# RWKV-7 recurrence in a hybrid block: v centred by the product that turns it, the two heads' u in two PSUM banks

## The chip, the cores and the metric

The kernel runs on one core of a Trainium2 chip. The metric is the device time of one execution in microseconds (us). A core has five engines that work side by side, each through its own instructions in order: PE (TensorE, matmuls; its weight loads are shown apart as PEld), DVE (VectorE), ACT (ScalarE), POOL (GpSimd) and SP (SyncE, which issues most loads). PE writes only to PSUM, which has eight banks; DVE and ACT read PSUM and copy results to SBUF.

## The reference, cut to what matters

The kernel computes a whole encoder block for 512 positions of 1024 channels: an input projection, an RWKV-7 branch and a gated linear recurrence side by side, their merge, attention over a fixed memory and a gated convolutional feed-forward network. The change lies in the RWKV-7 branch. It has 8 heads of 64 channels, and per head a state S of 64x64 that is carried from position to position:

```
state = state * w_t + sa b_t^T + v_t k_t^T        with sa = state a_t
y_t   = state r_t
mean  = mean(y); var = mean((y - mean)^2)
y     = (y - mean) * rsqrt(var + eps) * lnx_g + lnx_b
```

Since y loses its mean over the 64 value channels directly afterwards, the kernel takes the mean out of v before the recurrence, and no mean of y is computed.

## The kernel before

The 512 positions are worked in 8 chunks of 64. The 8 heads stand as 4 pairs (`NPAIR`, index j); of a pair, head e = 0 lies in partitions 0 to 63 and head e = 1 in 64 to 127 (`half[e]`). For a chunk c, all within-chunk products of keys, queries and the inverse of the chunk's triangular system have been prepared in `AK` and `BZ`. What is left is a chain from chunk to chunk (`chunk`):

- `UV` holds for each head, stacked over the partitions, the state in one half and the centred v in the other. `x` = `UV` times `AK` (L756), copied by DVE to `Xs` (L759).
- `u` = `BZ` times `Xs` (L769). It replaces the state in `UV`: for head 0 by an ACT copy (L771), for head 1 by a DVE copy (L772).
- `s` = `KBr` times `UV` (L778) and a second part of `y` (L783; the first, L763, needs `x`'s operands only).
- `Sn` is `s` with its decay (L788); `Sn` plus the decayed old state goes into the next chunk's `UV` (L792), and the next `x` may start. `SP` prepares the decay one chunk ahead (L799).

Beside the chain, `rows_v` turns the next chunk's v from channels to rows, so that it can stand in `UV`: for head 0 by four products with the identity (L729), for head 1 by four transposes (L727), into one PSUM tile in bank "kv". DVE sums each row (`vm`, L731) and subtracts the mean while it copies into `UV` (two instructions, L734). `rows_kb` turns the keys (`kbr`, L743), in bank "kv" for head 0 and bank "s" for head 1, and ACT copies them (L744). The recurrence has four PSUM banks of its own: "kv", "xu" (x, then u), "y" and "s".

The order of the instructions of each engine is worked out when the program is built, by a planner with expected durations. The recurrence has the highest priority there, and where it is expected to wait, PE is given products of the input projection (`in_ps`, L160 to L162, each 512 columns wide) that are left. `pin` (`keep_in_program_order`) keeps the DVE instructions of the chain in the order of the code. In the finished program each engine takes its instructions in that order, and an instruction waits for its operands. Between the recurrence's products stand also the gates of the linear recurrence (`ga` and `gx`, L850, L852) and products of the group norm (`gv`, `gg`). When projection and recurrence are done, `yb_ps` follows.

An f32 product that isn't a transpose appears in the trace as two records on PE, a transpose as one. So the 8 products of `u` are "x16", and four products of v "x8".

Of the kernel before, what the change touches and what calls it, by code (L numbers as in the profile page):

```python
# [9 lines left out]
F32 = mybir.dt.float32  # L10
F32R = mybir.dt.float32r
AF = mybir.ActivationFunctionType
ALU = mybir.AluOpType
AX = mybir.AxisListType
# [3 lines left out]
P = 128  # L18
# [5 lines left out]
HD = 64  # L24
NC = T // HD
NPAIR = NH // 2
# [27 lines left out]
def hybrid_block_kernel(ctx: ExitStack, tc: tile.TileContext, xT_d, mT_d, pv_d, cst_d, win_d, wk_d, wv_d,  # L54
                        lup_d, gup_d, rga_d, rgx_d, wba_d, wbb_d, wmix_d, wq_d, wo_d, wfi_d, wfo_d, out_d):
    nc = tc.nc
    V, S, PE = nc.vector, nc.scalar, nc.tensor
# [12 lines left out]
    def mm_ps(name):  # L70
        return pmm.tile([P, T], F32, tag="mm", name=name)

    def rw_ps(name, pool=None, tag="rw", **kw):
        return (pool or prw).tile([P, T], F32, tag=tag, name=name, **kw)
# [4 lines left out]
    ident = cst[:, 0:P]  # L79
    bones = cst[:, P:2 * P]  # L80
    smask = cst[:, 2 * P:2 * P + T]
    scmask = cst[:, 2 * P + T:]
# [184 lines left out]
    with tc.tile_pool(name="p0", bufs=1, reuse_waits="tile") as p0:  # L267
# [36 lines left out]
        for m in range(KB):  # L304
            ps = rw_ps(f"k_ps{m}") if 3 <= m < 6 else mm_ps(f"k_ps{m}")
# [174 lines left out]
    BZ = pa.tile([P, NPAIR * NC, P], F32, tag="AR", name="BZ")  # L480
    KBt = big.tile([P, NPAIR, 2 * NC + 1, HD], F32, tag="x16", name="KBt")
    vT = pa.tile([P, NPAIR, T], F32, name="vT")
# [23 lines left out]
    half = (slice(0, HD), slice(HD, P))  # L506
# [25 lines left out]
    for i in range(2):  # L532
        hs, oh = half[i], half[1 - i]
# [137 lines left out]
    for e in range(2):  # L671
        o = HD * e
# [5 lines left out]
    for g in range(4):  # L678
        e, i0 = divmod(16 * g, 32)
        o = HD * e  # L680
# [8 lines left out]
        for i in range(16):  # L689
            PE.matmul(pso[o:o + 32, i * 32:(i + 1) * 32], Hs[k:k + 32, i, :], ZA[k:k + 32, 1 - e, i0 + i, :],  # L690
                      start=True, stop=True)
        V.tensor_copy(BZ[o:o + 32, i0:i0 + 16, 32:64], pso[o:o + 32].rearrange("p (i t) -> p i t", t=32))
    for e in range(2):
        o = HD * e
# [9 lines left out]
    ch = ch_ctx.enter_context(tc.tile_pool(name="ch", bufs=1, reuse_waits="tile"))  # L704

    gup = ch.tile([P, T], F32, name="gup")
    nc.scalar.dma_start(gup, gup_d)


    yT = vT  # L710
    j3 = lambda a: a.rearrange("p (j i) -> p j i", i=HD)
    pin = tc.keep_in_program_order

    def ch_ps(name, tag):
        return pch.tile([P, T], F32, tag=tag, name=name)

    def rows_v(c):

        UV = ch.tile([P, 2, NPAIR, HD], F32, tag="UV", name=f"UV{c}", bufs=2)
        ps = ch_ps(f"vr{c}", "kv")  # L720
        for e in range(2):
            hs, oh = half[e], half[1 - e]
            for j in range(NPAIR):
                o = ps[oh, j * HD:(j + 1) * HD]
                src = vT[hs, j, c * HD:(c + 1) * HD]
                if e:
                    PE.transpose(o, src, ident[hs, hs])  # L727
                else:
                    PE.matmul(o, src, ident[hs, hs], start=True, stop=True)  # L729
        vm = ch.tile([P, NPAIR], F32, tag="vm", name=f"vm{c}", bufs=2)  # L730
        pin(V.tensor_reduce(vm, j3(ps[:, 0:256]), AX.X, ALU.add))  # L731
        for e in range(2):
            oh = half[1 - e]
            pin(V.scalar_tensor_tensor(UV[oh, e], vm[oh].unsqueeze(2).to_broadcast([HD, NPAIR, HD]), -1.0 / HD,  # L734
                                       j3(ps[oh, 0:256]), ALU.mult, ALU.add))
        return UV

    def rows_kb(c):
        KBr = ch.tile([P, 2, NPAIR, HD], F32, tag="KBr", name=f"KBr{c}", bufs=2)
        for e in range(2):  # L740
            ps = ch_ps(f"kbr{c}_{e}", ("kv", "s")[e])
            for j in range(NPAIR):
                PE.transpose(ps[:, j * HD:(j + 1) * HD], kb_cols(j, e, c), ident[half[e], half[e]])  # L743
            S.copy(KBr[:, e], j3(ps[:, 0:256]))  # L744
        return KBr

    def pc_b(c):
        return PC[:, :, c].unsqueeze(2).to_broadcast([P, NPAIR, HD])

    def chunk(c, UV, KBr, SP):  # L750
        last = c == NC - 1
        nUV = nKB = None
        psx = ch_ps(f"x{c}", "xu")
        for j in range(NPAIR):
            for e in range(2):
                PE.matmul(psx[half[e], j * HD:(j + 1) * HD], AK[:, e, j * NC + c, 0:HD], UV[:, e, j, :],  # L756
                          start=True, stop=True)
        Xs = ch.tile([P, NPAIR, HD], F32, tag="Xs", name=f"Xs{c}", bufs=2)
        pin(V.tensor_copy(Xs, j3(psx[:, 0:256])))  # L759
        psy = ch_ps(f"y{c}", "y")  # L760
        for j in range(NPAIR):
            for e in range(2):
                PE.matmul(psy[half[e], j * HD:(j + 1) * HD], UV[:, e, j, :], AK[:, e, j * NC + c, HD:P],  # L763
                          start=(j == 0), stop=False)
        psu = ch_ps(f"u{c}", "xu")
        for j in range(NPAIR):
            for e in range(2):
                hs = half[e]
                PE.matmul(psu[hs, j * HD:(j + 1) * HD], BZ[hs, j * NC + c, 0:HD], Xs[hs, j, :],  # L769
                          start=True, stop=True)  # L770
        S.copy(UV[half[0], 0], j3(psu[half[0], 0:256]))  # L771
        pin(V.tensor_copy(UV[half[1], 1], j3(psu[half[1], 0:256])))  # L772
        if not last:
            nUV = rows_v(c + 1)
            pss = ch_ps(f"s{c}", "s")
            for j in range(NPAIR):
                for e in range(2):
                    PE.matmul(pss[half[e], j * HD:(j + 1) * HD], KBr[:, e, j, :], UV[:, e, j, :],  # L778
                              start=True, stop=True)
        for j in range(NPAIR):  # L780
            for e in range(2):
                hs = half[e]
                PE.matmul(psy[hs, j * HD:(j + 1) * HD], UV[hs, e, j, :], BZ[hs, j * NC + c, HD:P],  # L783
                          start=False, stop=(j == NPAIR - 1))
        if not last:
            nKB = rows_kb(c + 1)
            Sn = ch.tile([P, NPAIR, HD], F32, tag="Sn", name=f"Sn{c}", bufs=2)
            pin(V.tensor_tensor(Sn, j3(pss[:, 0:256]), pc_b(c), ALU.mult))  # L788
            for e in range(2):
                hs = half[e]  # L790
                if c:
                    pin(V.tensor_tensor(nUV[hs, e], Sn[hs], SP[hs], ALU.add))  # L792
                else:
                    pin(V.tensor_copy(nUV[hs, e], Sn[hs]))
        if c < NC - 2:
            SP = ch.tile([P, NPAIR, HD], F32, tag="SP", name=f"SP{c}", bufs=2)
            for e in range(2):
                hs = half[e]
                V.tensor_tensor(SP[hs], nUV[hs, e], pc_b(c + 1)[hs], ALU.mult)  # L799
        S.copy(yT[:, :, c * HD:(c + 1) * HD], j3(psy[:, 0:256]))  # L800
        return nUV, nKB, SP

    with tc.high_priority(offset=1000000):
        UV, KBr, SP = rows_v(0), rows_kb(0), None
        for e in range(2):
            V.memset(UV[half[e], e], 0.0)
        for c in range(NC):
            UV, KBr, SP = chunk(c, UV, KBr, SP)
# [142 lines left out]
    for m in range(KB):  # L951
        xin = pm.tile([P, T], F32, tag="xin", name=f"xin{m}")
        nc.scalar.dma_start(xin, xT_d[:, m, :])
        ps = mm_ps(f"mix_ps{m}")
# [115 lines left out]
    for m in order:  # L1070
        ps = mm_ps(f"co_ps{m}")
# [87 lines left out]
    for m0 in range(0, FB, NQ):  # L1159
# [25 lines left out]
        for m in ms:  # L1185
            s = pc.tile([P, T], F32, tag="s", name=f"fs{m}")
# [228 lines left out]
```

## Time and profile before

| | |
|---|---|
| median of three runs | 916.9 us (916.62 to 917.09) |
| the profiled execution | 917.18 us, of which the span of the program is 915.4 |
| granted TensorE clock, mean | 0.997 of full speed |
| busy share of the span | PE 98%, PEld 85%, DVE 76%, ACT 55%, POOL 14% |
| DMA | 200 MB, 219 GB/s on average |

A busy share is a mean over the whole span. PE's records overlap, so that PE counts as busy also where its products are spaced wider than they need to be; the start times and the chain show that, not the share.

### The profile page before, as it was taken

The page shows a single profiled execution, that of the slowest core. Times are in us where ns is not written, and L with a number is a line of the kernel's source. Part 1 is how long each engine was busy: PE and PEld are TensorE (multiplying, and loading weights), DVE is VectorE, ACT ScalarE, POOL GpSimd, SP SyncE. Part 2 cuts the span into 40 slices and gives each one's busy share as a digit, 9 for nine tenths or more (in the row PEclk, how much of TensorE's full clock was granted, in tenths as well). Part 3 has the DMA queues.
Part 4 walks back from the last instruction along what each step waited for, and adds up shares of the span by engine and source line. Part 5 has one row for each costly group of instructions (what it writes and reads, how often), then busy time and mean ns, then how long its engine had stood idle before and what let it go on. Part 6 is the DMA issues. An engine that isn't in the chain of part 4 may idle for free.

```text
span 915.4 us, 15846 instructions
## 1 busy us (share of the span) xinstructions
PE 896.7 (98%) x6186; PEld 777.7 (85%) x6186; DVE 695.9 (76%) x1119; ACT 505.2 (55%) x763; POOL 129.5 (14%) x159
## 2 busy tenths in 40 slices
PE   6999999999999999999999999999999999999996
PEld 6888877788867677787887778999999999999996
DVE  7884698767956687776566568789897889999674
ACT  7674666532335465333454456666565556767663
POOL 0102222010012211001111211111111111201100
PEclk9999999999999999999999999999999999999998
DMA  8778889576499975558878958899989998998962
GB/s 277 281 268 224 182 235 209 167 185 182 138 218 246 186 170 128 181 188 221 226 216 204 183 134 194 234 272 271 260 251 290 262 302 249 250 274 212 280 199 92
DMA packets 102410, 200.06 MB, mean 219 GB/s; under 512 B 25344, under 2 KB 36736, under 8 KB 102272
## 3 DMA queue, kind: packets, MB, share of 16 engines
q1 hardware_dynamic: 69504, 119.75, 40.1%
q0 software_dynamic: 25504, 67.38, 36.0%
q10 hardware_dynamic: 7328, 11.92, 3.8%
q8 instruction: 48, 0.79, 0.3%
q14 instruction: 26, 0.21, 0.1%
HBM read 187.75 MB, written 77.59 MB: 290 GB/s over the span
## 4 chain that ended last, share of the span: by engine, by line
PE 81%; DVE 9%; DMA 6%; ACT 2%; issue 1%; SPq 0%; DVEq 0%; ACTq 0%
PE in_ps L160 5%; PE in_ps L161 5%; PE in_ps L162 5%; PE fx_ps L160 5%; PE fx_ps L162 5%; PE fx_ps L161 5%; PE fyz_ps L160 3%; PE fyz_ps L162 3%; PE fyz_ps L161 3%; DMA wfo_r<-dOs 2%; PE mix_ps L160 2%; PE co_ps L160 2%; PE mix_ps L161 2%; PE mix_ps L162 2%; PE co_ps L162 2%; DMA Nm<-dM 2%
## 5 line engine op out<-in xcount | busy, mean ns | idle before, releaser
L126 ACT CAST wfi_h<-wfi_r 128x1024 fp32r<-128x1024 f32 x77 | 81.0, 1052 | 78.1 <-PE fx_ps L161 23.8
L160 PE MATMUL in_ps<-hT,win_h 128*128 128x512 f32 x304 | 122.6, 404 | 0.8 <-DVE pr L525 0.6
L161 PE MATMUL in_ps<-hT,win_h 128*128 128x512 f32 x304 | 122.0, 403 | 0.0
L162 PE MATMUL in_ps<-hT,win_l 128*128 128x512 f32 x304 | 121.1, 399 | 0.0
L127 DVE TENSOR_TENSOR wfi_l<-wfi_r,wfi_h 128x1024 fp32r<-128x1024 f32 x77 | 94.0, 1221 | 23.9 <-ACT wfi_h L126 23.8
L425 POOL DMA_DIRECT2D dS<-in_wfi x66 | 66.6, 1038 | 271.9 <-PE in_ps L160 125.4
L114 ACT CAST win_h<-win_r 128x1024 fp32r<-128x1024 f32 x38 | 39.8, 1048 | 72.8 <-PE in_ps L161 64.7
L115 DVE TENSOR_TENSOR win_l<-win_r,win_h 128x1024 fp32r<-128x1024 f32 x38 | 46.4, 1221 | 32.1 <-ACT win_h L114 32.1
L160 PEld LDWEIGHTS in_ps<-hT,win_h 128*128 128x128 f32 x304 | 57.0, 187 | 15.5 <-DVE pr L525 1.1
L161 PEld LDWEIGHTS in_ps<-hT,win_h 128*128 128x128 f32 x304 | 57.0, 188 | 14.5 <-issue 1.2
L162 PEld LDWEIGHTS in_ps<-hT,win_l 128*128 128x128 f32 x304 | 57.0, 187 | 14.1 <-issue 0.5
L461 POOL DMA_DIRECT2D dOs<-in_wfo x54 | 40.0, 800 | 185.9 <-PE fx_ps L160 51.4
L1242 DVE TENSOR_TENSOR wfo_l<-wfo_r,wfo_h 128x1024 fp32r<-128x1024 f32 (+1 forms) x39 | 47.1, 1208 | 14.1 <-ACT wfo_h L1241 13.9
L1241 ACT CAST wfo_h<-wfo_r 128x1024 fp32r<-128x1024 f32 (+1 forms) x39 | 40.4, 1038 | 28.3 <-PE oyz_ps L161 9.5
L160 PE MATMUL fx_ps<-hq,wfi_h 128*128 128x256 f32 x176 | 49.8, 283 | 0.0
L162 PE MATMUL fx_ps<-hr,wfi_l 128*128 128x256 f32 x176 | 49.7, 283 | 0.0
L160 PE MATMUL fx_ps<-hr,wfi_h 128*128 128x256 f32 x176 | 49.7, 282 | 0.0
L160 PE MATMUL ox_ps<-go,wfo_h 128*128 128x256 f32 x176 | 49.6, 282 | 0.0
L160 PE MATMUL fyz_ps<-hq,wfi_h 128*128 128x256 f32 x176 | 49.4, 281 | 0.0
L161 PE MATMUL fx_ps<-hr,wfi_h 128*128 128x256 f32 x176 | 49.4, 280 | 0.0
L162 PE MATMUL ox_ps<-go,wfo_l 128*128 128x256 f32 x176 | 49.3, 280 | 0.1
L161 PE MATMUL ox_ps<-go,wfo_h 128*128 128x256 f32 x176 | 49.3, 280 | 0.0
(418 smaller groups left out, 2728.8 us busy)
## 6 DMA issues: line engine op xcount, KB each, us to landing
dS<-in_wfi POOLq DMA_DIRECT2D x66, 512.0 KB, 8.3
wfi_r<-dS SPq DMA_DIRECT2D x44, 512.0 KB, 6.4
win_r<-in_win SPq DMA_DIRECT2D x38, 512.0 KB, 5.0
wfi_r<-in_wfi SPq DMA_DIRECT2D x33, 512.0 KB, 5.6
dS<-dS POOLq DMA_DIRECT2D x22, 512.0 KB, 6.0
dOs<-in_wfo POOLq DMA_DIRECT2D x12, 512.0 KB, 7.4
wv_r<-in_wv SPq DMA_DIRECT2D x8, 512.0 KB, 5.2
dG<-gs ACTq DMA_DIRECT2D x16, 256.0 KB, 3.0
```

What stands on the lines that cost most here:

```text
L114: S.copy(hi[:, o:o + n], raw[:, o:o + n])
L115: V.tensor_tensor(lo[:, o:o + n], raw[:, o:o + n], hi[:, o:o + n].bitcast(F32), ALU.subtract)
L126: S.copy(hi, raw)
L127: V.tensor_tensor(lo, raw, hi.bitcast(F32), ALU.subtract)
L160: first = PE.matmul(ps, lh, rh, start=start, stop=False, **kw)
L161: PE.matmul(ps, lh, rl, start=False, stop=False, **kw)
L162: PE.matmul(ps, ll, rh, start=False, stop=stop, **kw)
L425: return lambda: nc.gpsimd.dma_start(s(out), src, **kw)
L461: yield lambda k=k, w=w, src=src: nc.gpsimd.dma_start(dO[n, m][:, k * P:(k + w) * P], src, **kw)
L1241: S.copy(hi[:, :n], raw[:, :n])
L1242: V.tensor_tensor(lo[:, :n], raw[:, :n], hi[:, :n].bitcast(F32), ALU.subtract)
```

## The change

Three edits. A matrix `centre` = identity - (1/64) x block of ones is built once by DVE, in place of the mask `scmask`, which is no longer needed by then. In `rows_v` both heads' v is multiplied by `centre` instead of being turned by the identity or a transpose; the result is turned and centred at once, and two ACT copies bring it to `UV`; the reduction `vm` and the two DVE instructions go. In `chunk`, `u` gets two PSUM tiles, head 0 in bank "xu" and head 1 in bank "s".

```diff
+    centre = scmask
+    V.scalar_tensor_tensor(centre, bones, -1.0 / HD, ident, ALU.mult, ALU.add)
...
         for e in range(2):
             hs, oh = half[e], half[1 - e]
             for j in range(NPAIR):
-                o = ps[oh, j * HD:(j + 1) * HD]
-                src = vT[hs, j, c * HD:(c + 1) * HD]
-                if e:
-                    PE.transpose(o, src, ident[hs, hs])
-                else:
-                    PE.matmul(o, src, ident[hs, hs], start=True, stop=True)
-        vm = ch.tile([P, NPAIR], F32, tag="vm", name=f"vm{c}", bufs=2)
-        pin(V.tensor_reduce(vm, j3(ps[:, 0:256]), AX.X, ALU.add))
+                PE.matmul(ps[oh, j * HD:(j + 1) * HD], vT[hs, j, c * HD:(c + 1) * HD], centre[hs, hs],
+                          start=True, stop=True)
         for e in range(2):
             oh = half[1 - e]
-            pin(V.scalar_tensor_tensor(UV[oh, e], vm[oh].unsqueeze(2).to_broadcast([HD, NPAIR, HD]), -1.0 / HD,
-                                       j3(ps[oh, 0:256]), ALU.mult, ALU.add))
+            S.copy(UV[oh, e], j3(ps[oh, 0:256]))
...
-        psu = ch_ps(f"u{c}", "xu")
+        psu = [ch_ps(f"u{c}_{e}", ("xu", "s")[e]) for e in range(2)]
         for j in range(NPAIR):
             for e in range(2):
                 hs = half[e]
-                PE.matmul(psu[hs, j * HD:(j + 1) * HD], BZ[hs, j * NC + c, 0:HD], Xs[hs, j, :],
+                PE.matmul(psu[e][hs, j * HD:(j + 1) * HD], BZ[hs, j * NC + c, 0:HD], Xs[hs, j, :],
                           start=True, stop=True)
-        S.copy(UV[half[0], 0], j3(psu[half[0], 0:256]))
-        pin(V.tensor_copy(UV[half[1], 1], j3(psu[half[1], 0:256])))
+        S.copy(UV[half[0], 0], j3(psu[0][half[0], 0:256]))
+        pin(V.tensor_copy(UV[half[1], 1], j3(psu[1][half[1], 0:256])))
```

## Rows read from the trace of the kernel before

**Rows 1.** The page's busy times, and its chain's shares by engine.
```profile
PE 896.7 (98%) x6186; PEld 777.7 (85%) x6186; DVE 695.9 (76%) x1119; ACT 505.2 (55%) x763; POOL 129.5 (14%) x159
...
PE 81%; DVE 9%; DMA 6%; ACT 2%; issue 1%; SPq 0%; DVEq 0%; ACTq 0%
```
**Rows 2.** Busy time of each engine in the recurrence's stretch.
```profile
core 0: us, PE busy (x) PEld busy (x) DVE busy (x) ACT busy (x) POOL busy (x), PEclk, DMA share, GB/s
287.70:359.60 71.90, 71.90 (x885) 50.80 (x884) 54.45 (x112) 34.98 (x65) 14.47 (x16) 1.00 0.78 164
```
**Rows 3.** Waits in that stretch: us in total, times, longest.
```profile
DVE UV L772 <- ACT UV L771: 3.4, 4, 1.5
PEld s L778 <- issue: 2.5, 6, 0.8
...
PEld s L778 <- ACT UV L771: 1.4, 4, 0.4
```
**Rows 4.** Timeline, weight loads of s: start, us, what [idle before, releaser].
```profile
306.39 0.19 PEld L778 LDWEIGHTS s<-UV,KBr 128*64 128x64 f32 x2 [0.36 <-ACT UV L771]
...
331.15 0.54 PEld L778 LDWEIGHTS s<-UV,KBr 128*64 128x64 f32 x14 [0.36 <-issue]
```
**Rows 5.** Chain in order of time, second chunk: start us, us, what.
```profile
304.01 0.60 PE vr L729 x8
304.62 0.34 PE vr L727 x4
...
305.57 0.43 PE in_ps L160
306.00 0.23 PE in_ps L161
...
306.46 0.26 PE s L778 x2
...
307.88 0.61 PE s L778 x14
...
310.15 0.40 PE kbr L743 x8
```
**Rows 6.** Chain in order of time, third chunk.
```profile
313.81 0.62 PE s L778 x16
...
315.04 0.39 PE kbr L743 x4
...
317.63 0.26 PE x L756 x2
317.89 0.12 PE y L763 x2
```
**Rows 7.** Chain: the first lone start of six, and the last chunk's.
```profile
297.32 0.26 PE s L778 x2
...
358.02 0.26 PE y L783 x2
```
**Rows 8.** Groups of instructions in the stretch: busy us, mean ns | idle before.
```profile
L734 DVE SCALAR_TENSOR_TENSOR UV<-vm,vr 64x256 f32<-64x256 f32 x16 | 6.7, 418 | 0.4
...
L236 ACT ACT_TABLE_LOAD x4 | 5.1, 1283 | 0.1
...
L731 DVE TENSOR_REDUCE vm<-vr 128x4 f32<-128x256 f32 x8 | 3.4, 425 | 1.0 <-PE vr L727 0.8
...
L771 ACT COPY UV<-u 64x256 f32<-64x256 f32 x8 | 2.9, 366 | 11.9 <-PE u L769 11.9
```
**Rows 9.** Timeline of DVE in the sixth chunk.
```profile
340.94 0.85 DVE L734 SCALAR_TENSOR_TENSOR UV<-vm,vr 64x256 f32<-64x256 f32 x2
341.72 0.41 DVE L788 TENSOR_TENSOR Sn<-s,PC 128x256 f32<-128x256 f32 x1
```
**Rows 10.** Timeline ahead of the recurrence (DVE) and behind it (PE's loads).
```profile
274.11 0.69 DVE L857 TENSOR_TENSOR xb<-xb,gx 128x512 f32<-128x512 f32 x1 [5.60 <-ACT gx L237]
...
366.59 0.19 PEld L161 LDWEIGHTS yb_ps<-yb,wbb_h 128*128 128x128 f32 x1 [0.84 <-DVE yb L907]
```

## The prediction, made before the result

> **What bounds the kernel now.** I read the page's totals and chain first [rows 1]. PE is busy for 98% of the span and holds 81% of the chain that ended last; DVE has 9% and ACT 2%. The change lies in the recurrence, so I next took its stretch, which its products fill from 287.7 to 359.6 us. In these 71.9 us PE is never without work, while DVE is busy for 54.45 us and ACT for 34.98 [rows 2]. The weight loads are busy for 50.80 us only, so the question is whether PE waits for somebody in the rest.
>
> The waits answer that [rows 3]. The gap of PE's loads before `s` is put down to ACT four times (1.4 us, the longest 0.4) and to nothing at all six times (2.5 us). In the timeline it is 0.36 us long behind a run of projection products whether ACT is named, as at 306.39, or nothing, as at 331.15 [rows 4]; only behind an f32 gate product is it longer. A gap that depends on what PE did before and not on who is named is PE's own change of work, not a wait for data. So in this stretch time goes where PE's instructions and their order put it, and neither the 1.27 us of DVE work per chunk that goes, nor a copy that ends sooner, is worth anything by itself. They count through the order, which was fixed when the program was built, around expected waits.
>
> The chain in order of time shows what an unlucky order costs [rows 5, 6]. Its three prices:
> A projection product behind recurrence work takes 0.43 us and one behind its like 0.23. So each projection interlude inside the recurrence costs 0.20; the stretch has 32 such 0.43 rows.
> `s` and its `y` start with one lone product each (x2, two records) of 0.26, and the other 14 records still take 0.61, as long as all 16 together (0.62). So a lone pair costs 0.26 + 0.26 = 0.52, less 0.02, and 0.20 for the interlude behind it: 0.70.
> The `kbr` transposes take 0.40 for all eight and 0.39 for four; splitting them costs 0.38.
>
> Why is `s` split? The DVE copy of u waits for the ACT copy, a wait that the rows show [rows 3], so between the two only the products of head 0 can run. This happens in six chunks from 297.32 on, and in the last, at 358.02, for `y` alone [rows 7].
>
> **The change part by part.**
> 1. *v by a product.* For head 0 the product is there already, with another right-hand side: no change. For head 1 four transposes, 0.34 us, become four products. The same shape of four takes 0.60 in the row before [rows 5], so the most is +0.26 a chunk, 8 x 0.26 = +2.1 us. If all of it ran two at a time, as the sixteen `s` records do (0.62, or 0.31 for eight [rows 6]), it would be -0.03 a chunk, -0.2 in all. Only the last product of one half and the first of the other are neighbours, so I take one slot of 0.15 off: +0.11 to 0.13 a chunk, **+1.0 us**.
> The Trainium skill (TensorE: Matmul & The Clock Gate, Terms) calls trn2's transpose mode four times faster for FP32. By that, four products would take 4 x 0.34 = 1.36 us and this term would be +8.2; the row of four products, 0.60, disagrees, and decides.
>
> 2. *DVE.* One reduction and two scalar_tensor_tensor per chunk go, 0.425 + 2 x 0.418 = 1.26 us, 8 x 1.26 = 10.1 us of 54.45 [rows 2, 8]. ACT gets two 64x256 copies from PSUM per chunk, 0.366 each by the copy of u: 5.9 us on 34.98. Both engines are covered by PE's work. Neither enters the sum directly; the cost without the cover is the slower rival below. What DVE's relief does to the order: behind the copy of u stood the reduction and the two centrings, and Sn started as the second of these ended (340.94 + 0.85 against 341.72 [rows 9]), so the planner had to fill that time. With Sn free to go when `s` ends, I expect one or two of the 32 interludes less per chunk, nine in all: **-1.8** (from 0 to 12 of them, -2.4).
>
> 3. *u in two banks.* The DVE copy no longer waits for the ACT copy (3.4 us in four waits [rows 3]). Bank "s", which now holds u of head 1, is freed by the DVE copy, so no `s` can start before it; the lone `s` pair goes. The lone pairs cost 6 x 0.70, and 0.26 + 0.20 in the last chunk: 4.7 us. What can remain is a lone `y` pair where ACT is done well before DVE, 0.46. All seven keeping it leaves a gain of 1.5, none 4.7. DVE often has another operation of 0.7 to 1.2 us in hand when u is ready, so I let half keep it: **-3.1**.
>
> 4. *`kbr`.* Its first half uses bank "kv", which v held until the centring; with the ACT copies it comes free well before "s", which is read by Sn. So halves that went together in four of eight cases will tend to be split: 4 x 0.38 = +1.5. Where the early half takes the place of an interlude 0.20 comes back. I take **+1.2** (0 to 1.5).
>
> 5. *x.* With less fill ahead of it, x may more often start with its first head alone, as at 317.63: 0.26 for x and 0.12 for y [rows 6]. At most three more, **+0.5** (0 to +1.2).
>
> 6. *Behind the recurrence*, PE does wait once: 0.84 at 366.59 for the split of yb on DVE [rows 10]. A recurrence that ends sooner thins DVE's and ACT's queues there: **-0.4** (0 to -0.8).
>
> 7. *`centre`* is one DVE operation of 128x128, between nothing and the 0.42 of the 64x256 form. The mask's last reader is past and DVE idles for 5.60 us before 274.11 [rows 10]. Nothing; without that cover 0.4.
>
> Sum: +1.0 - 1.8 - 3.1 + 1.2 + 0.5 - 0.4 = -2.6 us. The profiled execution took 917.18 (span 915.4 and 1.8 around it), so 914.6 for it, with a span of 912.8; the median of the runs is 0.3 lower, 916.9, and gives **914.3**. All bounds at their best give -0.2 - 2.4 - 4.7 + 0 + 0 - 0.8 = -8.1, at their worst +2.1 + 0 - 1.5 + 1.5 + 1.2 + 0 = +3.3.
>
> **Rivals.**
> *No difference.* The order's gain and PE's extra work cancel: lone `y` pairs stay in all chunks (-1.5), interludes fall by four only (-0.8), products cost +2.1, `kbr` +1.2: +1.0, 917.9. For it speaks that PE is the bound and gets more to do; against it the seven lone pairs. It also covers the case that the change does not do what it says: if the DVE copy waits for the ACT copy over UV, which both write, and not over u, two banks leave the wait, term 3 is 0 and the sum +0.5: 917.4. The rows don't tell the two apart.
> The Trainium skill (PSUM — Partial Sum Buffer, "PSUM bank collisions raise a hardware error") has reads by two engines collide per bank and quadrant of 32 partitions; by that the chip doesn't need this wait, as the two copies read different partitions, and it is the program's. No row here shows whose rule it is.
> Chance of no difference 0.27, of which 0.07 for the wait that stays.
>
> *A larger gain.* The plan of a chunk shortens so far that most interludes inside it go: 20 of 32 instead of nine, 2.2 us more, and no lone pair stays, 1.6 more: 910.5. Against it, every chunk keeps at least the waits for Xs, for u and for Sn. Chance 0.09.
>
> *Slower, through ACT.* The next x and the `kbr` transposes now wait for v's copies on ACT, which works in order and has four table loads of 1.28 us in the stretch [rows 8]. A pair of copies caught behind one comes up to 1.28 + 2 x 0.37 = 2.0 us late, and PE with its fixed order stalls for what its fill doesn't cover. From three full hits on, 6.0 us against the 2.6 gained, the kernel is slower: 920.3. For it, ACT is loaded unevenly; against it, ACT is half idle and v is not needed until Sn and the additions are done, well over 1 us later. Chance 0.13, with 0.03 more for terms at their worst (918.7 or more) and for products that cost four times a transpose (922): 0.16.
>
> **Numbers.** The forecast itself has 0.48. Under 0.2%, 1.8 us, a measurement of this kernel hardly tells a change from none. Faster: 0.48 + 0.09 = 0.57; same 0.27; slower 0.16. The range takes in no difference and part of the larger gain, and leaves out the full hits on ACT: 911.5 to 918.0. The forecast's own is 911.5 to 915.0.
>
> **What would show it.** The changed profile should show: v as 16 records in 1.05 to 1.2 us with no transposes; no x2 of `s`, and x2 of `y` before it in about half of the chunks; the waits of the copy of u for ACT gone; `kbr` mostly in fours; about 23 rows of 0.43 in the recurrence; its last product some 8 to 10 us earlier, as projection work moves behind it. The prediction is wrong if the lone pairs stay, or if gaps before PE's loads appear that exceed 0.36 us and name ACT.

## The result, and the profile after

The changed kernel takes 911.41 us (median of seven runs, 908.63 to 914.03) against 917.09 (seven runs, 916.31 to 919.38): a ratio of 0.9932, interval 0.9911 to 0.9953, so 4.3 to 8.2 us faster. Forecast were 914.3 and a range down to 911.5. The direction was right, the gain of 5.7 us a little over twice the 2.6 forecast, and the median lies just under the range.

The profiled execution took 914.03 us, the slowest of its seven; its span is 912.2. Line numbers after the change: v's products L727, ACT's copies of v L731, `kbr` L739, `x` L752, first part of `y` L759, `u` L765 with its copies L767 (ACT) and L768 (DVE), `s` L774, second part of `y` L779, `Sn` L784. The page of the changed kernel, busy times and the chain's shares:

```profile
PE 891.4 (98%) x6218; PEld 775.6 (85%) x6218; DVE 687.1 (75%) x1096; ACT 510.9 (56%) x779; POOL 129.3 (14%) x159
...
PE 88%; DMA 5%; DVE 4%; ACT 2%; issue 1%; SPq 0%; DVEq 0%; ACTq 0%
```

Beside [rows 1], PE has 32 records more (four transposes of one record became four products of two, in eight chunks) and is busy 5.3 us less: more work, done closer together. The busy times of the changed kernel from v's first product to the recurrence's last (columns as in [rows 2]):

```profile
286.79:342.00 55.21, 55.18 (x871) 41.21 (x871) 39.56 (x80) 35.55 (x75) 9.58 (x11) 1.00 0.71 154
```

The recurrence now ends at 342, where before it ended at 359.5: 17 us earlier, not the 8 to 10 that the prediction named. What used to fill it, projection products, now runs behind it in one block. Next the waits of the changed kernel while the recurrence runs (us in total, times, longest), and the chain in order of time for two of its chunks:

```profile
DVE UV L768 <- PE u L765: 6.0, 5, 1.8
...
ACT UV L731 <- PE vr L727: 1.6, 3, 0.8
...
PEld s L774 <- issue: 1.1, 3, 0.4
```

```profile
311.09 0.39 PE kbr L739 x4
311.48 0.43 PE in_ps L161
311.91 0.23 PE in_ps L162
312.14 0.44 PE u L765 x10
312.57 0.05 PE vr L727
312.63 0.06 PE u L765 x2
...
312.75 0.57 PE vr L727 x13
313.32 0.43 PE in_ps L160
...
314.46 0.61 PE s L774 x16
315.07 0.61 PE y L779 x16
```

Three things are to be seen. The DVE copy of u waits for PE only; the wait for the ACT copy [rows 3] is gone, so that wait was over `u` and not over UV. `s` runs as one x16 everywhere, and no lone pair of `s` stands before it. And `u` with `v` behind it takes 1.18 us (312.14 to 313.32), where [rows 5] has 1.56 for the same pair (304.01 to 305.57): v's products start before u's last, and v adds 0.57 here to u's 0.61.

To see where the stretch's time went, PE's weight loads are taken in order of start, from v's first to the first of `yb_ps`, and each is given the time to the start of the next. Summed by what they load (us; in brackets how many separate groups they stand in; both kernels have the same 99 projection and `gv` products there; the sums are good to some 0.05, as starts are read to 0.01). Where two classes are mixed, as in a v that runs into a `y`, the time goes to whichever load started last:

| | before | after | difference |
|---|---|---|---|
| projection and `gv` | 29.89 (35) | 27.13 (21) | -2.76 |
| `u` and v | 12.36 | 10.10 | -2.26 |
| `s` | 5.82 (13) | 4.31 (7) | -1.51 |
| second `y` | 6.63 | 5.67 | -0.96 |
| `x` and first `y` | 10.20 | 9.56 | -0.64 |
| `kbr` | 4.71 (12) | 6.48 (18) | +1.77 |
| f32 gates and `gg` | 7.57 | 7.87 | +0.30 |
| stretch | 77.18 | 71.12 | -6.06 |

The stretch also began 1.25 us earlier (286.79 against 288.04), so `yb_ps` starts at 357.91 instead of 365.22, 7.3 us earlier. Of these, 4.1 were lost again in this execution, since its span is only 3.2 us shorter; over the seven runs the median keeps 5.7. Waits of PE's loads behind the recurrence, in the changed kernel, and a row each of ACT and DVE there:

```profile
PEld sc_ps L1009 <- ACT ex L1016: 2.7, 3, 2.0
PEld yb_ps L160 <- DVE mB L910: 1.6, 2, 1.1
```

```profile
470.00 1.05 ACT L987 CAST K<-kvK 128x1024 fp32r<-128x1024 f32 x1 [3.07 <-DMA kvK<-dK]
...
471.08 1.23 DVE L988 TENSOR_TENSOR K<-kvK,K 128x1024 fp32r<-128x1024 f32 x1 [2.78 <-ACT K L987]
```

In attention ACT stands in front of a cast whose keys have not landed, DVE in front of the step that takes the cast's result, and the mask and exponentials of the scores come behind both. In the kernel before, the waits of `sc_ps` for `ex` come to 0.7.

### The profile page after: what moved, and what is told of

It is laid out like the page before. It is cut to its first block, busy times and chain, and to the rows that moved or that the text cites. A ratio compares the mean times of both kernels' runs of the same rounds, so it can differ in the third digit from the quotient of the medians.

```text
span 912.2 us, 15916 instructions
## 1 busy us (share of the span) xinstructions
PE 891.4 (98%) x6218; PEld 775.6 (85%) x6218; DVE 687.1 (75%) x1096; ACT 510.9 (56%) x779; POOL 129.3 (14%) x159
## 4 chain that ended last, share of the span: by engine, by line
PE 88%; DMA 5%; DVE 4%; ACT 2%; issue 1%; SPq 0%; DVEq 0%; ACTq 0%
PE in_ps L160 7%; PE in_ps L162 7%; PE in_ps L161 7%; PE fx_ps L161 5%; PE fx_ps L160 5%; PE fx_ps L162 5%; PE fyz_ps L161 3%; PE fyz_ps L162 3%; PE fyz_ps L160 3%; DMA wfo_r<-dOs 2%; PE mix_ps L160 2%; PE co_ps L160 2%; PE mix_ps L161 2%; PE mix_ps L162 2%; PE co_ps L162 2%; PE co_ps L161 2%
```

## The experiments

**The changed kernel again.** Unchanged, for how far its executions repeat.

> The changed kernel once more, as the measure for the others. Both theories: 911.4 us, between 908.6 and 914.0, and from v's first product to the first yb product 71.1 us (77.2 before).

Measured: 911.56 (five runs, 909.87 to 915.07), 0.9939 [0.9926, 0.9952]. The stretch is 71.17, its classes within 0.11 us of the table's. The span behind the start of `yb_ps`, 554.6 us, is again long (before 550.2, after 554.3), with 3.5 us of waits of `sc_ps` for `ex`, the longest 2.8 at 474.42. Just behind that wait the granted clock is 0.50 (the level of 1.2 GHz) from 474.66 to 478.07, and 1.00 (2.4 GHz) again after it; the execution before has no such stretch there. This too was the slowest execution of its set. So the gain of the stretch repeats to 0.05 us, and what comes back later is a matter of the execution.

**Each part alone.** `centre_alone` puts both u back into one bank of the changed kernel; `banks_alone` gives the kernel before two banks and leaves v to the transposes and DVE.

```diff
 centre_alone, against after
-        psu = [ch_ps(f"u{c}_{e}", ("xu", "s")[e]) for e in range(2)]
+        psu = [ch_ps(f"u{c}", "xu")] * 2
 banks_alone, against before
-        psu = ch_ps(f"u{c}", "xu")
+        psu = [ch_ps(f"u{c}_{e}", ("xu", "s")[e]) for e in range(2)]
...
```

> The product with centre and the ACT copies, but u in one bank as before. Theory of the order (the gain is PE's own time: lone starts, interludes, overlap of v's and u's products): the lone starts of s and y come back in seven chunks, 0.26 us each for s and y, the overlap and most of the saved interludes stay; the stretch is 73.5 to 75 us, the kernel 914 to 915.5. Rival (the gain is the 10 us of VectorE work taken off the chain): 911.5, the stretch as in the changed kernel.

> u in two banks, v turned and centred as before. Theory of the order: no lone s, s and y together about 2 us cheaper, v and u as dear as before (12.4 us in the stretch), about as many interludes as before; stretch 74.5 to 76, kernel 914.5 to 916. Rival (the second bank gives the whole gain): 911.5. Rival (VectorE work off the chain gives it): 917, no change.

Measured: `centre_alone` 916.41, 0.9985 [0.9970, 1.0000]; `banks_alone` 916.56, 0.9998 [0.9987, 1.0008]. Both missed what was expected of them (914 to 915.5 and 914.5 to 916). Alone, the banks are worth nothing measurable, and the centring 1.4 us at the edge of the noise; together they are worth 5.7 us. The stretch by class, as differences to before:

| | projection | `u`, v | `s` and second `y` | `kbr` | `x`, first `y` | gates, `gg` | stretch |
|---|---|---|---|---|---|---|---|
| centre_alone | -2.67 | -1.26 | -0.07 | +1.54 | -0.31 | +1.10 | -1.66 |
| banks_alone | +0.24 | +0.18 | -2.29 | +0.76 | +0.08 | +0.64 | -0.39 |
| both (after) | -2.76 | -2.26 | -2.47 | +1.77 | -0.64 | +0.30 | -6.06 |

This tells which edit makes what. The interludes go with the centring: rows of 0.43, counted in each kernel from v's first product up to and with the block of projection behind the recurrence, fall from 32 to 23 in `centre_alone`, rise to 38 in `banks_alone`, and are 19 with both. The lone `s` pairs go with the banks. The chain of `centre_alone` around `s` in the first chunk, and that of `banks_alone` in the fifth:

```profile
293.89 0.26 PE s L774 x2
294.15 0.26 PE y L779 x2
294.41 0.43 PE in_ps L162
294.83 0.61 PE s L774 x14
```

```profile
331.05 0.61 PE u L769 x16
331.66 0.43 PE in_ps L162
...
332.78 0.26 PE y L783 x2
333.03 0.61 PE s L778 x16
```

With one bank PE still issues a lone pair and then projection. With two banks and DVE still busy centring, `s` is whole, but PE is given projection there all the same.

**v of head 1 by transposes again**, in the changed kernel, to price the prediction's first term by itself; it is not centred then.

```diff
...
+                if e:
+                    PE.transpose(o, src, ident[hs, hs])
+                else:
+                    PE.matmul(o, src, centre[hs, hs], start=True, stop=True)
```

> The changed kernel, but head 1's v is turned by transposes and not centred (its output is not the reference's). Theory of the order with overlap: transposes don't overlap with the other head's products nor with u, so v and u together cost 1 to 2 us more than the 10.1 of the changed kernel, and the kernel is 0.5 to 2 us slower than that. The prediction's term (products dearer than transposes): 1.0 us faster than the changed kernel.

Measured: 915.62, 0.9987 [0.9974, 0.9999], 4.2 us above the changed kernel's 911.41, twice the most that was expected. `u` and v take 13.32 us instead of 10.10, in 27 groups instead of 14; the other classes add up to 1.1 more. The planner's order changed with the edit, so this is the price of the transposes together with the places they got. The chain of this kernel in its first chunk:

```profile
292.26 0.60 PE vr L732 x8
292.86 0.28 PE vr L730 x3
293.15 0.60 PE u L769 x8
293.75 0.17 PE vr L730
293.93 0.60 PE u L769 x8
294.53 0.43 PE in_ps L160
```

The row to look at is `u`: its eight products, 0.61 as one x16, take 0.60 twice here, with a transpose between. That is what two groups of four products of one head cost side by side (as `vr L732 x8`); that the order has put them so is inferred from this price, since the rows don't name heads. v and u of this chunk take 2.27 us.

**DVE's work put back**, as three pinned instructions a chunk whose result nobody reads, v still by products and ACT.

```diff
+        vm = ch.tile([P, NPAIR], F32, tag="vm", name=f"vm{c}", bufs=2)
+        dd = j3(smask[:, 256:512])
+        pin(V.tensor_reduce(vm, j3(smask[:, 0:256]), AX.X, ALU.add))
+        for e in range(2):
+            oh = half[1 - e]
+            pin(V.scalar_tensor_tensor(dd[oh], vm[oh].unsqueeze(2).to_broadcast([HD, NPAIR, HD]), -1.0 / HD,
+                                       j3(smask[oh, 0:256]), ALU.mult, ALU.add))
```

> The changed kernel with as much idle VectorE work put back in the old place of the order: per chunk one reduction and two scalar_tensor_tensor of the same sizes, on an SBUF constant, their results unused. Theory that VectorE's relief counts through the order: more interludes (about 25 instead of 21), stretch 72 to 73.5 us, kernel 912.5 to 914. If the relief is worth nothing (overlap and banks are the whole gain): 71.1 and 911.5. If VectorE's time is on the chain as such: 10 us back, about the 917 of before.

Measured: 919.59, 1.0022 [1.0010, 1.0035]. In the stretch it does about what was expected: 73.49 us, 2.4 more than the changed kernel, with 26 rows of 0.43 instead of 19 and no lone `s`; five projection products fewer stand in it (94), so with equal work it would be some 1.2 longer (an estimate, at 0.23 each). The kernel as a whole lost more than three times that, and the 912.5 to 914 expected was missed. Its v starts at 290.57 (286.79 in the changed kernel), its span behind `yb_ps` is 555.8. Part of the latter can be seen in DVE, in PE's loads and in the row of the stretch that follows (columns as in [rows 2]):

```profile
371.07 0.69 DVE L917 TENSOR_TENSOR mB<-yb_ps,gb 128x512 f32<-128x512 f32 x1 [3.89 <-DMA gb<-dG]
...
373.02 0.29 PEld L157 LDWEIGHTS gv<-gv_l,bonesr 128*128 128x128 f32 x1 [2.86 <-DVE gv_l L155]
...
372.63:376.04 3.41, 3.02 (x7) 2.44 (x8) 2.98 (x6) 2.13 (x4) 0.00 (x0) 0.50 0.34 83
```

DVE stands before the multiplication by a gate that has not landed; the split `gv_l` comes behind it in DVE's order, and PE's loads wait 2.86 us for it. At its end the granted clock falls to 0.50 (1.2 GHz) for 3.41 us, and seven loads stand 0.43 apart instead of 0.23: wait and clock together some 4.3 us (an estimate from these rows). The mean granted clock of eight of the twelve executions is 0.994 to 0.996, and of one in seven of the changed kernel. So part of the 8 us is a late transfer and the lower clock behind it, and not DVE's time as such; why the gate lands late and v starts late was not found.

**The order within v, and `kbr` kept whole.** `v_by_turns` issues the heads' products alternately. `kbr_together` holds `kbr` back until `Sn` has read its bank, so that it isn't split. `both` has both.

```diff
 v_by_turns, against after
-        for e in range(2):
-            hs, oh = half[e], half[1 - e]
-            for j in range(NPAIR):
+        for j in range(NPAIR):
+            for e in range(2):
+                hs, oh = half[e], half[1 - e]
 kbr_together, against after
...
-            nKB = rows_kb(c + 1)
...
-            pin(V.tensor_tensor(Sn, j3(pss[:, 0:256]), pc_b(c), ALU.mult))
+            sn = pin(V.tensor_tensor(Sn, j3(pss[:, 0:256]), pc_b(c), ALU.mult))
+            nKB = rows_kb(c + 1, sn)
```

> The changed kernel with v's products of the two heads by turns (head 0, head 1, head 0, ...) as u's are, instead of four and four. Theory of overlap: products of the two heads in different quarters of the array run two at a time only as neighbours, so sixteen records of v alone take 0.61 us instead of 0.89, and v and u in the stretch 8 to 9 us instead of 10.1; kernel 909.5 to 911. If the order of the two heads is no matter: 10.1 and 911.5.

> The changed kernel, but the first kbr transposes wait for Sn too, so that both heads' run together. Theory (splitting costs 0.38 each): kbr 4.7 us instead of 6.5 in the stretch, given back in part where the early half was fill (one or two interludes more); kernel 909.5 to 911.5. Rival (the early half is free fill): 912 or more.

> v by turns and kbr together in the changed kernel. If the prices add: stretch 68 to 69.5 us, kernel 908 to 910. If the order changes against it: 911.5 or more.

Measured: 909.99 (908.88 to 911.60), 0.9918 [0.9904, 0.9932]; 910.93, 0.9931 [0.9906, 0.9956]; 909.97, 0.9926 [0.9908, 0.9945]. The stretches are 70.15, 69.45 and 68.82 us against 71.12. By turns, `u` and v take 8.89 us, 1.2 less (in one chunk 0.3 of it is a wait of `s` that stands behind v); kept whole, `kbr` takes 3.62, 2.9 less, of which the gates and `gg` (+1.2) and others give some back. In time the three can't be told from one another, and their intervals overlap that of the changed kernel. The chain of `v_by_turns`, v by itself and v behind u:

```profile
288.33 0.61 PE vr L727 x16
...
312.95 0.44 PE u L765 x10
...
313.56 0.29 PE vr L727 x11
313.86 0.43 PE in_ps L162
```

The same eight products of v take 0.61 by turns and 0.89 in fours (`286.86`, below); behind u they add 0.30 by turns (312.95 to 313.86 is 0.91, less 0.61).

**Products in the kernel before**, centred by DVE as ever, in fours and by turns: the edit of v's products alone, with the identity in place of `centre`.

```diff
 products_only, against before
...
-                if e:
-                    PE.transpose(o, src, ident[hs, hs])
-                else:
-                    PE.matmul(o, src, ident[hs, hs], start=True, stop=True)
+                PE.matmul(ps[oh, j * HD:(j + 1) * HD], vT[hs, j, c * HD:(c + 1) * HD], ident[hs, hs],
+                          start=True, stop=True)
```

> The kernel before, with head 1's transposes of v replaced by products with the unit matrix and nothing else: VectorE still centres, the two u still share a bank. If products in two quarters of TensorE's array overlap and transposes do not, v and u of a chunk get shorter: their 12.4 us of the stretch before become 10 to 11, and the kernel is 1 to 2.5 us faster (914.5 to 916). By the prediction's term, products cost more than transposes, the kernel is about 1.0 slower (918).

> As products_only, with the products of the two heads issued by turns instead of four and four. If overlap between neighbours in different quarters is what counts, v and u take 8.5 to 9.5 us of the stretch and the kernel is 2.5 to 4 us faster than before (913 to 914.5). If the order within the eight does not matter, it stands at the time of products_only; by the prediction's term at 918.

Measured: `products_only` 919.28, 1.0028 [1.0015, 1.0041]; `products_by_turns` 913.96, 0.9962 [0.9949, 0.9975]. By turns came out as expected: `u` and v 9.04 us. In fours the expectation failed: 11.81 instead of 10 to 11, a gain of 0.55, and the kernel was slower. The chain of `products_only` shows one reason, v in pieces:

```profile
310.01 0.37 PE vr L724 x4
310.39 0.26 PE x L752 x2
310.64 0.12 PE y L759 x2
310.76 0.37 PE vr L724 x6
311.13 0.55 PE x L752 x13
...
312.21 0.49 PE vr L724 x6
312.70 0.43 PE in_ps L160
...
328.26 0.89 PE vr L724 x16
```

The three pieces take 0.37 + 0.37 + 0.49 = 1.23 us, v whole 0.89. The rest of the 0.95 us by which this stretch is longer than before (78.13): seven lone `s` pairs instead of six, more interludes (its 97 projection products stand in 37 groups), and a wait of 1.00 us for `yb` ahead of the first `yb_ps`, which is 0.22 in the kernel before.

**Where v stands.** Two kernels in which only the planner's freedom is cut: `products_behind_u` is `products_only` with v held behind u; `v_behind_s` is the changed kernel with v held behind `s`.

```diff
+                if after is not None and e == 0 and j == 0:
+                    tc.add_manual_dep(ins.ins, after.ins.name, mybir.DependencyInfo(
+                        mybir.DependencyClass.NoSync, mybir.DependencyReason.DATA), reason="place of v")
...
 products_behind_u
-            nUV = rows_v(c + 1)
+            nUV = rows_v(c + 1, un)
```

> As products_only, with v's products held back until u's eight are issued, so that in every chunk they stand directly behind u. If what v costs hangs on what stands beside it, u and v take 1.18 us a chunk as in the changed kernel, 9.8 us in the stretch (7 x 1.18, 0.89 for the first v, 0.61 for the last u) against 11.8 in products_only, and the kernel is 2 us or more faster than products_only: 915 to 917.5. If the price of v is its own, wherever it stands, u and v stay at 11.8 and the time near 919.

> The changed kernel, with v's products held back until s's eight are issued, so that they stand between s and y instead of behind u. If the overlap with u is what made v cheap, u and v rise from 10.1 to about 12 us of the stretch (8 x 0.89 and 8 x 0.61), and the kernel loses about 2 us: 913 to 914. If v is as cheap beside s and y, u and v stay near 10 us and the time at 911 or less.

Measured: `products_behind_u` 915.06, 0.9983 [0.9974, 0.9993], 4.2 us faster than `products_only`, with `u` and v at 9.83 us, as worked out (9.8). `v_behind_s` 912.64, 0.9953 [0.9935, 0.9970]; `u` and v 9.84, the stretch 71.18. So the place of v, and not the kind of instruction alone, sets its price; nor does it take the second bank, which `products_behind_u` hasn't. But the neighbour need not be u. The chain of `v_behind_s`:

```profile
303.50 0.62 PE s L776 x16
304.12 0.72 PE vr L727 x13
304.83 0.11 PE y L782 x3
304.95 0.00 PE vr L727
```

v begins to overlap with the `y` behind it. The explanation "behind u" falls; "whole, and beside recurrence products that it can share PE with" stands.

## Why the prediction was wrong

**The step that failed is the first, v by a product: +1.0 (from -0.2 to +2.1) was forecast, and `u` with v took 2.26 us less.** The terms that lie in the stretch (all but the -0.4 behind it) add up to -2.2; it came out at -6.06, and of the 3.9 between, 3.3 are this term. Two things were wrong in it. First, the overlap. The prediction let one slot of 0.15 overlap between the heads; the chain has, in the changed kernel,

```profile
286.86 0.89 PE vr L727 x16
```

so 1.20 - 0.89 = 0.31, two slots, and a whole v costs 0.05 less than the 0.60 + 0.34 of products and transposes in [rows 5]. Second, and more: v was priced as if it stood alone. In five chunks it stands directly behind u and adds 0.36 to 0.58, by overlap that a price of v alone doesn't hold; even -0.2, the bound for full pairing, left this out. The trace of the kernel before shows it in one place that the prediction didn't use, the third chunk, where v's products of head 0 were mixed with u:

```profile
311.63 0.31 PE vr L729 x3
311.95 0.11 PE u L769 x3
...
312.35 0.06 PE u L769 x3
312.42 0.34 PE vr L727 x4
```

The four products and u take 0.79 us there (311.63 to 312.42), where alone they take 0.60 and 0.61; the four transposes behind them take their full 0.34. The experiments bear out both points: transposes for head 1 alone cost 3.22 us in `u` and v, products put into the old order save only 0.55, and held behind u 2.53. That order and neighbours carry most of the term is thereby shown; why transposes don't share PE in the rows of the kernel before (four take 0.34, two 0.23, whatever is beside them) isn't.
The Trainium skill (TensorEngine Tiling (Array Packing), Key Properties) states that tiles of the array run loads and products in parallel; by its table (64×64 Mode), u and v of the two heads stand in four different tiles. Rows agree: 0.61 by turns against 0.60 for half as many of one head. The Trainium skill's rule that trn2's transpose mode is four times faster for FP32 (TensorE: Matmul & The Clock Gate, Terms), weighed in the prediction at +8.2, doesn't hold for these tiles: four products take 0.60 and four transposes 0.34, and the term came out at -2.26.

**DVE's relief and the two banks (terms 2 and 3)** were right in mechanism and nearly in size. Their sum was -4.9 for interludes and lone pairs; projection, `s` and second `y` together lost 2.76 + 2.47 = 5.23. Rows of 0.43 fell by 13, from 32 to 19, where nine were forecast. A lone `y` pair stayed in four chunks, close to the half allowed, and in two of them it takes 0.12 and 0.20 instead of 0.26, since v runs beside it. What the prediction treated as two sums is one: `centre_alone` takes nine rows of 0.43 away, just the nine forecast, but leaves the lone `s`; `banks_alone` takes the lone `s` away and gives six interludes back. Had the banks been added alone, the stretch would have gained 0.4 us and not the 3.1 of term 3.

**`kbr`** measured +1.77 where +1.2 was forecast and 1.5 the bound: all sixteen halves now stand apart. **x** measured -0.64 instead of +0.5; lone `x` pairs went from four to three. The gates and `gg`, not in the sum, took 0.30 more. **Behind the recurrence** the wait for the split of yb was to shrink by 0.4. It didn't move from the 0.84 of [rows 10], though the recurrence ended 17 us earlier:

```profile
359.28 0.19 PEld L161 LDWEIGHTS yb_ps<-yb,wbb_h 128*128 128x128 f32 x1 [0.84 <-DVE yb L903]
```

**The rivals.** That the wait of the copy stays is refuted by the waits above. *No difference* rested on products at +2.1. *Slower through ACT* didn't happen: ACT is busy 35.55 us of 55.21, waits for v's products and not they for it, and the longest gap of PE's loads in the recurrence that names ACT is 0.37, a hundredth over the 0.36 that the prediction reads as PE's own change of work. *A larger gain* was nearest in time (910.5), by another road: 13 interludes went, not 20, and lone `y` pairs stayed. That its time lies so near is luck: the term of v made up for what the order did not give.

**What stays open.** The later loss of 4.1 us in the profiled execution lines up with waits for keys and a mask in attention and `yb_ps`. `again` has the attention part too, and the lower clock behind it; the profiles of `v_by_turns` and `kbr_together`, whose recurrence ends as early, have 0.7 us of it and 549.7 us behind `yb_ps`. So it isn't a fixed price of an earlier end, but what decides it in an execution was not tried. Nor was why the gate lands late in `dve_load_back`, and what the load costs without that.

## What to carry to other kernels

Where PE is always busy and an order is fixed ahead, price an added product by what will stand beside it, not by its row alone: small products of different halves of the partitions share PE, and eight of them cost 0.89, 0.61, 0.57 or 0.30 us by order and neighbour. Two edits that each free one end of the same gap may be worth little alone and much more together, so cost them as a pair. Issue the two heads' products by turns: products in that order, without the rest of the change, took the kernel before to 913.96 where the same products in fours took it to 919.28, and with the change it stands at 909.99, which can't be told from the 911.41 in fours.

## What the runs showed that was not expected

- Replacing transposes by products made PE's part shorter, though it holds more records: `u` and v 13.32 us with transposes, 10.10 with products, in otherwise the same kernel.
- v cut into three pieces takes 1.23 us and whole 0.89, much as `kbr` in halves takes 0.39 twice and in one piece 0.40.
- One class of PE's work can be cut by 2.9 us (`kbr_together`) and the stretch gain only 1.7: f32 gate and `gg` products beside it took 1.2 more.
- The stretch repeats to 0.05 us between two executions (71.12 and 71.17), while the executions of the same kernel spread from 908.63 to 915.07.
- A single wait of 2.8 or 2.9 us on PE (in `again` and `dve_load_back`) goes with 3.41 us at a granted clock of 0.50 at or behind its end, in a kernel that otherwise stands at 1.00 from its start-up to its last microseconds.
